# A streaming encoder layer: three groups' down products behind a block's last feature, some down weights split as units of their own, and a final norm at half the spacing

## The chip, the cores and the metric

The kernel runs on one core of one Trainium2 chip. A core has TensorE (PE, the matmul array; PEld is its weight load), VectorE (DVE), ScalarE (ACT), GpSimd (POOL) and SyncE (SP, which here issues nearly all DMAs). They run side by side and wait for each other through semaphores. The metric is device time in microseconds (us) of one execution; lower is better. Three runs of the kernel before gave 2262.98, 2264.62 and 2265.98 us.

## The reference

One layer over 2048 prompt frames and 64 sample frames of width 1024: a norm, an input projection, a gated delta rule on one half of the columns and pooling on the other, an output projection, and a feed-forward part with a last norm. The change touches the feed-forward part and the last norm alone:

```python
def rmsnorm(x, w):
    xf = x.astype(jnp.float32)
    y = xf * lax.rsqrt(jnp.mean(xf * xf, axis=-1, keepdims=True) + EPS)
    return (y * w.astype(jnp.float32)).astype(x.dtype)
...
    h = rmsnorm(x, norm2_w)
    x = x + (jax.nn.silu(h @ w_gate) * (h @ w_up)) @ w_down
...
    y_prompt = rmsnorm(hp, normf_w)
    y_sample = rmsnorm(hs, normf_w)
```

`w_gate` and `w_up` are 1024 x 2816, `w_down` is 2816 x 1024. Frames lie along the free axis of the tiles, model width along the 128 partitions.

## The kernel before, in words

**An order planned ahead.** The kernel text does not issue instructions. Each call is noted by a `Machine` (line 64), which knows an estimated duration for each and at the end (`issue`, line 189) puts all of them in a fixed order for each engine by a list schedule: of what is ready by the estimate, the lowest rank first. The rank is the place in the program text; `machine.boost` moves it forward (`HURRY` by 400 places). A tile of a pool has a tag with a number of buffers; who asks for one too many gets a buffer when the estimate says that its last reader is done. Small side jobs are generators (`Chain`, line 395): each `yield x` lets the next step come `x` us of estimated TensorE time later, and `pump()` between matmuls runs the steps that are due.

**Stages.** The first part of the kernel (to about 940 us) makes the delta-rule and pooling halves, the output projection and the residual x, kept in DRAM as `x2d`. The second part is the feed-forward stage, in three blocks of 704 frames (`NB2`, b = 0, 1, 2), each seen as two halves of 352. The 2816 columns of gate and up are 22 features f of 128 (`NF`), in six groups of 4, 4, 4, 4, 2 and 4 (`FGROUPS`, gi = 0 to 5).

**A feature** (`gate_up`, line 1695) computes gate and up for the two halves at once, with seven products (a Strassen scheme over gate/up rows, frame halves and width halves) in place of eight. Each product is 4 x 3 matmuls of 352 columns: operands are split in two float16 parts, and three cross products are summed. ScalarE copies products out of PSUM (`g`, `u`), VectorE adds others, ScalarE makes the sigmoid in three steps (`hr`), VectorE multiplies. The result is the tile `hr`, with `HRAW` buffers. For groups that go on in Strassen form, ScalarE also sums squares of the result (`esq`).

**A group's down product.** When a group's last feature is done, `factors` (line 1763) takes a scale from the squares (the small matmul `ec`), forms four sums per pair of features (`q`, on GpSimd; on VectorE for the last pair of a block) and splits seven factors per pair in two float16 parts, a ScalarE and a VectorE instruction each. They are put in the tile `hq` of the tag `op`, which has two buffers. `down_strassen` (line 1788) then runs, for each weight unit m, seven products (`dx`, `dy`, `dz`), and VectorE adds each into the tiles `y` (eight tiles, one buffer each, loaded from `x2d` by `new_y`). Units: four for a 4-group, two for the 2-group. In block 0 the groups 0 and 4, and in block 2 the group 5, are done without Strassen in float32r (`plain`, line 570; `down`, line 1751; the split features are then `h3l`, also of the tag `op`).

**Order of the work.** The list `order` (lines 573 to 576) is walked by the main loop (line 1824): feature after feature, and the down products of group gi behind feature `f0 + G + LATER` for the first `LASTD` groups, behind the block's last feature for the others. With `LATER, LASTD = 1, 4` (line 1890) groups 0 to 3 come behind features 5, 9, 13 and 17, groups 4 and 5 behind feature 21.

**Weights.** `plan` lists the weight units in order of use, and `weights_ahead` (line 788) keeps up to four ready. A unit takes buffers of two rings of four (`wsp`, `wsp2`; tiles `ws...` for gate/up, `wsd` for down). In block 0 each gate/up unit is loaded, summed on GpSimd, squared and split on ScalarE and VectorE (`prep_strassen`), and its parts are stored (`due`, `stored`); blocks 1 and 2 load the parts. `prep_down` (line 742) does the same for a Strassen down unit. For groups 1, 2, 3 and 5 the sums were made in the first part of the kernel (`summed`). For the groups 0 and 4, which are plain in block 0, nothing is ready in block 1: the unit's first use there loads two pieces (`wrdt`, `wrdl`), takes squares, a scale (the small matmul `wd`), four GpSimd sums (`wrda`, `wrdb`) and the splits into `wsd`, and stores them (`dn<-wsd`). Block 2 loads them (`wsd<-dn`).

**Between blocks.** `load_h` loads and splits the next block's normed input (`hA`, `hB`). `between` (line 1816) is a chain: the final norm of the block just done (`final_norm`, line 1627, through `rstd`, line 861, and `put_y`, line 1636, which scales y on VectorE and stores it to `out_yT`), then `new_y` for the next block, then the norm statistics of the block after. The steps of the final norm are `LAT_STAT` = 1.63 us apart: for each of two halves eight sums of squares, a pause, and eight stores. The last block has its own `last_norm`.

Of the kernel before, what the change touches and what calls it, by code (L numbers as in the profile page):

```python
# [9 lines left out]
F16 = mybir.dt.float16  # L10
# [8 lines left out]
P = 128  # L19
# [22 lines left out]
N2 = TB2 // 2  # L42
# [329 lines left out]
def hybrid_kernel(ctx, tc, a, o):  # L372
    nc = machine = Machine(tc.nc)
# [74 lines left out]
    cpool, wpool, opool = pool("cpool"), pool("wpool"), pool("opool")  # L448
# [22 lines left out]
    psg = psmm  # L471
# [26 lines left out]
    groups, f0 = [], 0  # L498
# [34 lines left out]
    plan, pres = [], []  # L533
# [12 lines left out]
    for j in range(NBLK):  # L546
        win = [("win", m) for m in range(21)]
        base = len(plan)
        at = 5 + 4 * OUT_AFTER
# [16 lines left out]
    def halves(b, gi):  # L566

        return ((0,), (1,)) if (b, gi) == (NB2 - 1, len(groups) - 1) else ((0, 1),)
# [9 lines left out]
    for op in order:  # L578
        if op[0] == "gu":
            plan.append(("gu", op[2]))  # L580
        else:
            plan += [("dn", m, *groups[op[2]]) for m in range(KT)] * len(halves(*op[1:])) if plain(*op[1:]) else [
                ("ds", m, *groups[op[2]]) for m in range(KT // 2 * groups[op[2]][1] // 4)]
    ready, due, stored = [], [], set()
    state = {"at": 0}
    flat = lambda t: t.rearrange("p q n -> p (q n)").bitcast(F32)
    wq = {}
# [8 lines left out]
    def wsplit(t, raw, n=512, eng=None):  # L596
        nc.scalar.copy(t[:, 0, :n], raw[:, :n])
        (eng or nc.vector).tensor_tensor(out=t[:, 1, :n], in0=raw[:, :n], in1=t[:, 0, :n].bitcast(F32), op=ALU.subtract)

    def prep():  # L600
        key = plan[state["at"]]
        state["at"] += 1
        if key[0] == "pre":
            if not state.get("sampled"):
                return plan.insert(next(i for i in range(state["at"], len(plan)) if plan[i][0] != "pre") + 1, key)
            return pre_sums(*key[1:])
        if key in stored and key[0] in wsd:
            parts = []
            for i in range(2):
                t = wtiles(f"p{i}")[1]()  # L610
                nc.sync.dma_start(out=flat(t), in_=wsd[key[0]][key[1], i])
                parts.append(t)
        elif key[0] == "wl":
            raw, parts = (f() for f in wtiles("l"))
            nc.sync.dma_start(out=raw, in_=wpd[key[1]] if key[2] else a["wout"][key[1]][:, :512])
            wsplit(parts, raw)
        elif key[0] in ("win", "wout"):
            parts = []
            for i in range(2):
                raw, t = (f() for f in wtiles(f"p{i}"))  # L620
                src = a[key[0]][key[1]][:, 512 * i : 512 * i + 512]
                nc.sync.dma_start(out=raw, in_=wpd[key[1]] if key[0] == "wout" and i else src)
                if key == ("win", 0):

                    r3, h3, l3 = (x.rearrange("p (k c) -> p k c", c=P) for x in (raw, t[:, 0], t[:, 1]))
                    nc.gpsimd.memset(l3[:, :, 64:].bitcast(F32), 0.0)
                    nc.scalar.copy(l3[:, :, :64], r3[:, :, :64])
                    nc.scalar.copy(h3[:, :, :64], r3[:, :, :64])
                    tt(h3[:, :, 64:], r3[:, :, 64:], l3[:, :, :64].bitcast(F32), ALU.subtract)
                else:  # L630
                    wsplit(t, raw)
                parts.append(t)
            if len(key) == 2:
                due.append((key, [(wsd[key[0]][key[1], i], t) for i, t in enumerate(parts)]))
        elif key[0] == "dn":
            _, m, f0, G = key
            raw, parts = (f() for f in wtiles("d", m % 2 == 0))
            nc.sync.dma_start(out=raw[:, : G * P], in_=a["wd"][m][:, f0 * P : (f0 + G) * P])
            wsplit(parts, raw, G * P, nc.vector)
        elif key[0] == "ds":  # L640
            parts = prep_down(key, *key[1:])
        else:
            parts = prep_strassen(key)
        ready.append((key, parts))

        while due and due[0][0] != key:
            k, done = due.pop(0)
            for dst, t in done:
                nc.sync.dma_start(out=dst, in_=t if t.dtype == F16 else flat(t))
            stored.add(k)  # L650
# [136 lines left out]

    def weights_ahead():
        while state["at"] < len(plan) and len(ready) < AHEAD + 1:
            if plan[state["at"]][0] in ("gu", "dn") and not wq:  # L790
                return
            prep()

# [64 lines left out]
        mm(ps, ones_r, hi, start=True, stop=False)  # L858
        mm(ps, ones_r, lo, start=False, stop=True)

    def rstd(tag, r, src, subs, pool, ttag, tbufs, eng, psg=psmm):

        for lo, n in subs:
            rs = r[:, lo : lo + n]
            for k in range(KT):
                x = src(k, lo, n)
                if k == 0:
                    act(rs, x, AF.Square)
                else:
                    sq = pool.tile([P, n], F32, tag=ttag, name=f"sq{k}{tag}{lo}", bufs=tbufs)  # L870
                    act(sq[:, :n], x, AF.Square)
                    eng.tensor_tensor(out=rs, in0=rs, in1=sq[:, :n], op=ALU.add)
                yield LAT_STAT
            yield WAIT_STAT
            ps = psg(f"rp{tag}{lo}")
            two = [pool.tile([P, n], F32R, tag=ttag, name=f"{nm}{tag}{lo}", bufs=tbufs)[:, :n] for nm in ("hi", "lo")]
            column_sums(ps[:, :n], rs, *two)
            act(rs, ps[:, :n], AF.Ln, bias=epsc, scale=1.0 / D)
            act(rs, rs, AF.Exp, scale=-0.5)
# [90 lines left out]
    for _ in range(PREPS):  # L970
        prep()
# [5 lines left out]
    at = 0  # L977
# [593 lines left out]
    hq = {}  # L1571

    def load_h(b, names):
        for nm in names:
            for k in range(4):
                t = hq[nm][k]
                if "pool" in wq:
                    raw = wq["pool"].tile([P, N2], F32, tag="t", name=f"xh{nm}{k}_{b}", bufs=TB)
                else:
# [12 lines left out]
    for k in (4, 5, 6, 7, 0, 1, 2, 3):  # L1592
        t = wpool.tile([P, 512], F32, tag="xc", name=f"od{k}", bufs=XBUFS["xc"])
# [19 lines left out]
    f2 = pool("f2", behind=True)  # L1613
# [13 lines left out]
    def final_norm(b, ys):  # L1627
        for i in range(2):
            rf = cpool.tile([P, TB2], F32, tag="r", name=f"rf{b}_{i}")
            src = lambda k, *_: ys[k][:, i]  # L1630
            yield from rstd(f"nf{b}_{i}_", rf, src, [(0, N2)], f2, "t", TB, nc.gpsimd)
            for k in range(KT):
                put_y(b, ys, k, i, rf)
                yield LAT_STAT

    def put_y(b, ys, k, i, rf):
        y = ys[k][:, i]
# [4 lines left out]
    def last_norm(b, ys, i, done):  # L1642
# [3 lines left out]
        def new(nm):  # L1646
            return f2.tile([P, 2, N2], F32, tag="hr", name=nm, bufs=HRAW).rearrange("p s n -> p (s n)")[:, :n] if n > N2 else tmp(nm)[:, :n]

# [37 lines left out]
    def tmp(nm):  # L1686
        return f2.tile([P, N2], F32, tag="t", name=nm, bufs=TB)

# [74 lines left out]
    def factors(b, gi):  # L1763

        f0, G = groups[gi]
        es = einv[b, gi] = f2.tile([P, 6], F32, tag="es", name=f"es{b}_{gi}", bufs=2)
        c = es[:, :1]
        scale_of(c, esq.pop((b, gi))[:, : 2 * G], 2 * G, 2.0**13, psp.tile([P, 512], F32, tag="mm", name=f"ec{b}_{gi}", bufs=PSM), "sqe")
        nc.vector.reciprocal(es[:, 1:2], c)
        t = opool.tile([P, 13 * G // 2, N2], F16, tag="op", name=f"hq{b}_{gi}", bufs=2)  # L1770
        for p in range(G // 2):
            f = f0 + 2 * p
            u, v = h3.pop(f), h3.pop(f + 1)
            low = f2.tile([P, N2], F16, tag="h7", name=f"h7{b}_{f}", bufs=4)
            part = {nm: (t[:, 13 * p + 2 * i], t[:, 13 * p + 2 * i + 1] if i < 6 else low) for i, nm in enumerate(FH)}
            gt = (nc.vector if f + 2 == NF else nc.gpsimd).tensor_tensor
            t3, t2, t4 = (tmp(f"q{i}{b}_{f}") for i in (3, 2, 4))
            for nm, x in (("11", u[:, 0]), ("21", v[:, 0]), ("22", v[:, 1])):
                split16(*part[nm], x, c)
            gt(out=t3, in0=v[:, 1], in1=u[:, 1], op=ALU.subtract)  # L1780
            gt(out=u[:, 1], in0=u[:, 1], in1=u[:, 0], op=ALU.subtract)
            gt(out=t2, in0=v[:, 1], in1=u[:, 1], op=ALU.subtract)
            gt(out=t4, in0=v[:, 0], in1=t2, op=ALU.subtract)
            for nm, x in (("T1", u[:, 1]), ("T2", t2), ("T3", t3), ("T4", t4)):
                split16(*part[nm], x, c)
            h3[f] = part
# [29 lines left out]
    def between(b):  # L1816
# [4 lines left out]
        if b + 2 < NB2:  # L1821
            yield from stats2(b + 2, f2, "t", TB)

    for op in order:
        b = op[1]
        if op[0] == "gu":
            f = op[2]
# [5 lines left out]
            gi = max(g for g, (f0, G) in enumerate(groups) if f0 <= f)  # L1833
# [14 lines left out]
        else:  # L1848
            f0, G = groups[op[2]]
# [36 lines left out]
LAT_SILU = 7.08  # L1886
LAT_STAT = 1.63
LAT_APPLY = 1.69
TB = 7
LATER, LASTD = 1, 4  # L1890
STATS0 = 0
ODB = 200
PREPS = 1
# [3 lines left out]

SLACK = 0.6
TINY = 1e-30
HRAW = 7  # L1900
HOT_ROWS = BOOST
HPOOL = (0, 1, 2, 3)
LAT_LOAD = 0.6
# [115 lines left out]
```

## Time and profile before

| | us |
|---|---|
| median of three runs | 2264.62 |
| lowest and highest | 2262.98, 2265.98 |
| the profiled execution | 2265.8 |
| its span, first to last instruction | 2264.0 |

Mean granted clock of TensorE over the span: 0.994 of full speed.

How to read it: nearly all instructions are recorded by one helper and so carry the line L286; groups are told apart by the names of their tiles, buffer numbers left out. Times in windows and in the chain are us from the span's start. A duration of a matmul in the profile includes its way through the array, and matmuls overlap: the distance from one start to the next is what counts, and the chain shows it. Waits are put down to what ended last.

### The profile page before, as it was taken

Reading aid. Unit: us, or ns where it says so; the run is one execution under the profiler, and the core shown is the slowest. Engines: PE = TensorE matmul, PEld = TensorE weight load, DVE = VectorE, ACT = ScalarE, POOL = GpSimd, SP = SyncE. Lnnn points to the kernel's source line nnn. Section 1 sums busy time; section 2 is a strip of 40 time slices with the busy share of each in tenths; the row PEclk is TensorE's granted clock in tenths of the full one; section 3 lists DMA queues with packets and bytes.
Section 4 is the critical chain, followed back from the end, with each engine's and each line's share of the span. In section 5 each row is a group of like instructions: output and inputs, shape, how many; then the busy total and the mean of one; then the engine's idle time right before and its main releaser. Section 6 shows DMA issues by size and latency. Waiting matters only on the chain. (4 is left out here: it accounts for less than half of the span.)

```text
span 2264.0 us, 41509 instructions
## 1 busy us (share of the span) xinstructions
PE 2207.0 (97%) x14763; PEld 1649.5 (73%) x14763; DVE 1611.4 (71%) x3198; ACT 1437.4 (63%) x3437; POOL 767.0 (34%) x869
## 2 busy tenths in 40 slices
PE   8999999999999999999999999999999999999998
PEld 8998898788878788758666676656666566666667
DVE  8988876685667887788998986666545756445647
ACT  6987876796768875687787775743533554423533
POOL 3425233443236551356444226342200152010102
PEclk9999999999999999999999999999999999999999
DMA  8765477657566667986686567487644576544442
GB/s 304 252 194 185 162 267 244 204 190 240 190 203 219 202 181 237 316 268 224 233 277 202 182 225 250 151 309 223 195 146 154 181 245 206 149 149 148 145 140 70
DMA packets 219392, 467.73 MB, mean 207 GB/s; under 512 B 27184, under 2 KB 88624, under 8 KB 219184
## 3 DMA queue, kind: packets, MB, share of 16 engines
q1 hardware_dynamic: 218608, 464.36, 63.3%
q8 instruction: 115, 1.88, 0.3%
q14 instruction: 93, 0.76, 0.1%
q10 hardware_dynamic: 576, 0.72, 0.1%
HBM read 336.77 MB, written 128.22 MB: 205 GB/s over the span
## 5 line engine op out<-in xcount | busy, mean ns | idle before, releaser
L286 PE MATMUL pp<-h,wsp 128*128 128x512 f32 (+1 forms) x2480 | 546.2, 363 | 8.6 <-DVE wsp L286 8.6
L286 PEld LDWEIGHTS pp<-h,wsp 128*128 128x128 f32 x2480 | 402.3, 189 | 57.4 <-ACT wsp L286 8.6
L286 PEld LDWEIGHTS <-wsd 128*128 128x128 f16 x2352 | 231.1, 99 | 143.1 <-issue 13.7
L286 PE MATMUL dx<-hq,wsd 128*128 128x352 f16 x1232 | 237.6, 316 | 9.5 <-ACT wsd L286 2.8
L286 PEld LDWEIGHTS <-ws11S 128*128 128x128 f16 x1584 | 153.4, 98 | 87.2 <-ACT ws11S L286 5.5
L286 PEld LDWEIGHTS <-wsS3S 128*128 128x128 f16 x1584 | 154.2, 98 | 85.0 <-issue 4.5
L286 PEld LDWEIGHTS <-wsS 128*128 128x128 f16 x1584 | 154.3, 98 | 84.3 <-issue 3.7
L286 DVE SCALAR_TENSOR_TENSOR y<-dx,es,y 128x352 f32<-128x352 f32 x240 | 135.3, 579 | 72.7 <-PE dx L286 68.2
L286 ACT COPY g<-px 128x352 f32<-128x352 f32 x132 | 58.3, 442 | 179.5 <-PE px L286 178.2
L286 PE MATMUL pz<-op,wsp 128*128 128x288 f32 (+1 forms) x768 | 163.0, 353 | 0.3 <-DVE op L286 0.3
L286 ACT ACTIVATE hr<-g,wscale 128x352 f32<-128x352 f32 x132 | 77.1, 584 | 134.9 <-DVE g L286 134.8
L286 POOL TENSOR_TENSOR q<-hr,hr 128x352 f32<-128x352 f32 x52 | 52.3, 1006 | 291.0 <-DVE hr L286 289.4
L286 PE MATMUL px<-hA,ws11S 128*128 128x352 f16 x792 | 137.3, 313 | 4.6 <-ACT ws11S L286 3.6
L286 ACT CAST TV_p<-pt_p 128x512 f16<-128x512 f32 x192 | 109.0, 588 | 42.0 <-PE pt_p L286 41.1
L286 PE MATMUL pz<-hA,wsS 128*128 128x352 f16 x792 | 134.4, 313 | 0.9 <-ACT wsS L286 0.8
L286 PE MATMUL py<-hA,wsS3S 128*128 128x352 f16 x792 | 134.3, 312 | 0.1
L286 PE MATMUL py<-hA,ws11S 128*128 128x352 f16 x792 | 132.8, 313 | 0.5 <-DVE hr L286 0.2
L286 PE MATMUL dy<-hq,wsd 128*128 128x352 f16 x672 | 129.7, 319 | 3.3 <-DMA out_yT_dram<-y 1.6
L286 PE MATMUL px<-hA,wsS 128*128 128x352 f16 x792 | 129.6, 312 | 2.1 <-ACT g L286 2.1
L286 PE MATMUL px<-hB,ws 128*128 128x352 f16 x792 | 129.5, 313 | 2.0 <-DVE u L286 2.0
L286 PE MATMUL px<-hA,wsS3S 128*128 128x352 f16 x792 | 129.6, 313 | 0.7 <-ACT g L286 0.6
L286 PEld LDWEIGHTS pz<-op,wsp 128*128 128x128 f32 x768 | 120.5, 188 | 12.6 <-DVE op L286 0.7
(755 smaller groups left out, 4940.5 us busy)
## 6 DMA issues: line engine op xcount, KB each, us to landing
wsp<-wnd SPq DMA_DIRECT2D x126, 512.0 KB, 3.8
ws11S<-g SPq DMA_DIRECT2D x44, 512.0 KB, 3.9
wsS3S<-g SPq DMA_DIRECT2D x44, 512.0 KB, 3.6
wsS<-g SPq DMA_DIRECT2D x44, 512.0 KB, 3.6
wnd<-wsp SPq DMA_DIRECT2D x42, 512.0 KB, 5.0
wsd<-dn SPq DMA_DIRECT2D x34, 512.0 KB, 3.5
xd<-x2d SPq DMA_DIRECT2D x96, 176.0 KB, 3.5
wsd<-dn SPq DMA_DIRECT2D x34, 384.0 KB, 3.5
```

Of the source, the lines that this page charges most:

```text
L286: getattr(getattr(self.nc, op.eng), name)(*args, **kw)
```

## The change

1. `LASTD` becomes 3: group 3's down products also come behind the block's last feature, ahead of those of groups 4 and 5. Group 4's factors in Strassen form get a tile of their own tag (`hq2`, one buffer), where a third `hq` would be needed. In block 0 group 4 is plain, and its split features stay in the tag `op`.
2. `plan` gets units `pd` behind some features of block 1: the four down units of group 0 behind features 0 to 3, the two of group 4 behind features 7 and 9 (`PREP_AT`). Such a unit is split and stored, and is not handed to TensorE; the unit's use later in block 1 loads it.
3. The final norm of blocks 0 and 1 steps at `PACE` = 0.8 in place of 1.63; the pause stays.
4. Buffers: the small tiles `t` have 8 in place of 7 (`TB`), the features' outputs 6 in place of 7 (`HRAW`).

No matmul is added or taken away.

```diff
     for op in order:
         if op[0] == "gu":
             plan.append(("gu", op[2]))
+            if op[1] == 1 and op[2] in PREP_AT:
+                gi, m = PREP_AT[op[2]]
+                plan.append(("pd", m, *groups[gi]))
...
+        elif key[0] == "pd":
+            key = ("ds", *key[1:])
+            prep_down(key, *key[1:])
+            return
         elif key[0] == "ds":
             parts = prep_down(key, *key[1:])
...
-            if plan[state["at"]][0] in ("gu", "dn") and not wq:
+            if plan[state["at"]][0] in ("gu", "dn", "pd") and not wq:
...
-    def rstd(tag, r, src, subs, pool, ttag, tbufs, eng, psg=psmm):
+    def rstd(tag, r, src, subs, pool, ttag, tbufs, eng, psg=psmm, pace=None):
...
-                yield LAT_STAT
+                yield pace or LAT_STAT
...
-            yield from rstd(f"nf{b}_{i}_", rf, src, [(0, N2)], f2, "t", TB, nc.gpsimd)
+            yield from rstd(f"nf{b}_{i}_", rf, src, [(0, N2)], f2, "t", TB, nc.gpsimd, pace=PACE)
             for k in range(KT):
                 put_y(b, ys, k, i, rf)
-                yield LAT_STAT
+                yield PACE
...
-        t = opool.tile([P, 13 * G // 2, N2], F16, tag="op", name=f"hq{b}_{gi}", bufs=2)
+        t = (f2.tile([P, 13, N2], F16, tag="hq2", name=f"hq{b}_{gi}", bufs=1) if G == 2 else
+             opool.tile([P, 26, N2], F16, tag="op", name=f"hq{b}_{gi}", bufs=2))
...
-TB = 7
-LATER, LASTD = 1, 4
+TB = 8
+LATER, LASTD = 1, 3
...
-HRAW = 7
+HRAW = 6
+PREP_AT = {0: (0, 0), 1: (0, 1), 2: (0, 2), 3: (0, 3), 7: (4, 0), 9: (4, 1)}
+PACE = 0.8
```

## The prediction

> **What bounds the kernel now.** I read the page first, for the share of each engine.
>
> ```profile
> span 2264.0 us, 41509 instructions
> PE 2207.0 (97%) x14763; PEld 1649.5 (73%) x14763; DVE 1611.4 (71%) x3198; ACT 1437.4 (63%) x3437; POOL 767.0 (34%) x869
> ```
>
> TensorE is the bound, and the change takes no matmul away. It can only win time in which TensorE waits or runs slowly. So I went on to the waits of TensorE, window by window over the feed-forward stage (from about 940 us), and kept the four places where they are dense. Columns: who waited, for whom, us in total, times, longest.
>
> ```profile
> PE dz L286 <- DVE y L286: 2.6, 1, 2.6
> PE dx L286 <- DVE hq L286: 0.6, 1, 0.6
> ...
> PE dx L286 <- ACT wsd L286: 2.8, 1, 2.8
> PE px L286 <- DVE u L286: 1.5, 1, 1.5
> PE dx L286 <- DVE wsd L286: 0.7, 1, 0.7
> ...
> PE ec L286 <- DVE sqe L286: 3.1, 1, 3.1
> PE dx L286 <- ACT hq L286: 1.4, 1, 1.4
> ...
> PE dy L286 <- DMA out_yT_dram<-y: 1.6, 1, 1.6
> PE dz L286 <- DVE y L286: 0.6, 1, 0.6
> ```
>
> The places are: the end of block 0 (1361 us on), the first down products of block 1 (1460 on), the end of block 1 (1789 on) and the first down products of block 2 (1910 on). A wait also has a second price, which the windows view shows (PE, PEld, DVE, ACT and POOL busy with counts, granted clock, DMA share, GB/s). Beside it stand one stretch from the chain that ended last, and two rows of the half-clock stretch itself.
>
> ```profile
> 1814.12 2.69 PE dx L286 x18
> ...
> 1361.00:1373.00 12.00, 8.32 (x38) 4.36 (x37) 10.50 (x20) 8.14 (x19) 8.22 (x10) 0.72 0.80 262
> 1367.00:1369.00 2.00, 2.00 (x8) 1.02 (x7) 2.00 (x6) 0.97 (x2) 2.00 (x3) 0.50 0.83 230
> 1460.00:1468.00 8.00, 6.33 (x42) 3.89 (x40) 8.00 (x15) 7.80 (x17) 1.04 (x2) 1.00 0.12 33
> 1474.00:1486.00 12.00, 8.13 (x35) 3.63 (x34) 11.87 (x19) 6.17 (x17) 8.12 (x8) 0.72 0.96 325
> 1789.00:1806.00 17.00, 11.62 (x63) 6.47 (x61) 16.83 (x41) 8.80 (x22) 0.00 (x0) 0.80 0.44 137
> 1910.00:1924.00 14.00, 11.13 (x74) 6.97 (x72) 9.77 (x18) 0.00 (x0) 0.03 (x1) 1.00 0.96 356
> ```
>
> 18 matmuls in 2.69 us is 0.149 us each when nothing waits. What a window lost is its length less its matmuls at 0.149: 12 − 38 × 0.149 = **6.3 us** at the end of block 0; 8 − 42 × 0.149 = 1.7 and 12 − 35 × 0.149 = 6.8, together **8.5**, at the start of block 1; 17 − 63 × 0.149 = 7.6 at the end of block 1, and 8 of those 63 are the `ec` column sums of hardly any length (the other 55 make 8.2 us), so I take **8.5**; 14 − 74 × 0.149 = **3.0** at the start of block 2. In sum 26.3 us. About half of it is the clock: in 1367 to 1369 TensorE is busy throughout and does 8 matmuls where 13 would fit, at a granted clock of 0.50.
>
> [...] Here the longest single wait before a halved clock was 2.6 us, with shorter ones just ahead, while 1910 to 1924 kept 1.00 through shorter waits; the measured windows decide, and they hold both prices already.
>
> **The change, part by part.** *Three groups' products behind the last feature.* The waits at the block ends come from the factors of the last group: they need the last feature's output, and only group 4's products cover them.
>
> ```profile
> 1781.00:1806.00 25.00, 19.62 (x116) 11.71 (x115) 24.67 (x56) 9.16 (x23) 0.00 (x0) 0.86 0.44 144
> ...
> L286 DVE SCALAR_TENSOR_TENSOR y<-dx,es,y 128x352 f32<-128x352 f32 x16 | 8.6, 576 | 0.0
> L286 DVE SCALAR_TENSOR_TENSOR hq<-hr,es,hq 128x352 f16<-128x352 f32 x8 | 4.1, 578 | 0.0
> ...
> L286 ACT ACTIVATE hq<-hr,es 128x352 f16<-128x352 f32 x8 | 4.0, 574 | 0.2 <-DVE es L286 0.2
> ...
> 2223.43 18.89 PE d L286 x117
> ```
>
> At block 1's end VectorE is busy 24.67 of 25 us. One weight unit of a Strassen down product is 7 products of 6 matmuls: 42 × 0.149 = 6.26 us for a unit of a 4-group, 7 additions into y at 8.6 / 16 = 0.54 us. Cover before: two units of group 4, twelve and a half us. After: four units of group 3 more, 25.0, in all 37.6 us. VectorE's work in it: 42 additions (22.6 us), the 14 splits of the factors (0.51 each, 7.2), some 3 us of sums and finishing: 33 us. It fits, ScalarE's 14 splits at 0.5 (7 us) fit far better, and TensorE has work throughout. I take the whole **8.5 us** there; bounds 0 and 8.5.
>
> At block 0's end the cover is 25.0 us of group 3 and group 4's plain products: 96 matmuls at 18.89 / 117 = 0.161, 15.5 us. But here the change adds a wait. The tag `op` has two buffers; group 3's factors and group 4's split features hold both, so the last group's 14 splits can only be written when TensorE has read group 3's factors for the last time. Their instructions on ScalarE and VectorE stand in an order fixed ahead, and what is queued behind them, the copies out of PSUM and the additions into y, would wait too if group 3 came late. From there 15.5 us remain, and VectorE has 7.2 us of splits and 16 additions (8.3 us at about 0.52, estimated from the 0.54 above): 15.5 against 15.5. The splits rank first, and nothing of the column sum is left to do then, so the first product should start in time and later ones wait a little. Bounds: 0 and 6.3 us left; I take 2 left, **4.3 won**. In blocks 1 and 2 group 4 has its own buffer, and nothing waits.
>
> The price is a run of eight features (14 to 21) without down products between. In blocks 1 and 2 that is free. In block 0 ScalarE and VectorE also split each feature's weights:
>
> ```profile
> 1311.00:1336.00 25.00, 25.00 (x176) 16.47 (x175) 20.51 (x41) 22.31 (x53) 6.48 (x7) 1.00 0.61 216
> ...
> L286 ACT ACTIVATE junk<-wr 128x512 bf16<-128x512 f32 x9 | 5.6, 622 | 5.2 <-DMA wr<-in_wg_dram 5.2
> L286 ACT CAST wsd<-wrd 128x256 fp32r<-128x256 f32 x7 | 2.7, 401 | 2.6 <-PE pz L286 1.3 <-PE py L286 1.3
> ...
> PE px L286 <- ACT ws11S L286: 1.8, 1, 1.8
> PE dx L286 <- ACT hq L286: 1.0, 1, 1.0
> ...
> 940.00:1025.00 85.00, 77.37 (x524) 49.29 (x523) 74.90 (x126) 76.70 (x174) 42.82 (x32) 1.00 0.86 297
> ```
>
> Two features (25 us) with the splits of two weight units take 22.3 us of ScalarE; in a steady run six more squares (0.62 each, 3.7) come and four casts for group 4 (1.6) go: about 24.5 of 25. Eight features are 100 us, two units are ready ahead (some 15 us of ScalarE saved), group 3's 14 splits come in (7). So ScalarE just keeps up, with some 10 us in hand over 100. The features' worst wait for weights in the rest of block 0 was 1.8 us. The bound from the other side is the run of six features at the stage's start: 85 − 77.4 = 7.6 us idle at this load with the stage change on top. I take 2 us new, less the 1.0 that TensorE now waits for group 3's factors: **1 us lost**; bounds 1 won and 7.6 lost. One buffer fewer for the features' outputs costs nothing: six hold one group and two features more.
>
> *Weights of groups 0 and 4 as units of their own.* Before, group 0's four units are made between feature 5 and their use; after, one behind each of features 0 to 3 of block 1, and loaded back.
>
> ```profile
> L286 POOL TENSOR_TENSOR wrda<-wrdt,wrdl x6: 727/773/1082, 1358.0 to 1516.0; 128x256 f32<-128x256 f32 x6
> L286 DVE SCALAR_TENSOR_TENSOR wsd<-wrdt,dscale,wsd x6: 741/752/1418, 1449.3 to 1769.2; 128x512 f16<-128x512 f32 x6
> dn<-wsd SPq DMA_DIRECT2D x6, 512.0 KB, 4.9
> wsd<-dn SPq DMA_DIRECT2D x34, 512.0 KB, 3.5
> ...
> 1396.00:1471.00 75.00, 73.22 (x499) 47.73 (x498) 44.01 (x83) 55.22 (x130) 31.18 (x35) 1.00 0.52 161
> ```
>
> A unit is four POOL sums (3.1 us), four splits on VectorE (about 3) and on ScalarE with two squares (about 4), two loads, two column sums, two stores. The 75 us before the stall have room for what is moved in: VectorE 44, ScalarE 55, POOL 31, DMA at 0.52. What is added is twelve loads (six of 512 KB, six smaller) in SP's queue at 3.5 us to landing, well ahead of use. With the weights there, the 2.8 and 0.7 us waits go; so does the congestion of VectorE (11.87 of 12 us). What may be late next is group 0's own factors; I leave 1.5 us. **7.0 us won**, bounds 0 and 8.5. Group 4's two units saw no wait, and moving them earlier gives nothing.
>
> *Final norm at half the spacing.* Two halves of 16 steps, each 0.83 us closer: 26.6 us sooner at the end.
>
> ```profile
> 1853.98 0.87 SPq L286 DMA_DIRECT2D out_yT_dram<-y  x2
> 1907.59 0.98 SPq L286 DMA_DIRECT2D out_yT_dram<-y  x2
> 1909.21 5.47 SPq L286 DMA_DIRECT2D y<-x2d  x6
> ```
>
> The last store goes out at 1907.6 and the next y is fetched at 1909 to 1915, while TensorE needs it from 1910. Stores at about 1881 free y long before: **3.0 us won**, bounds 0 and 3.0. In block 1 y is late too, behind the late weights, and this edit is what keeps it from being the next wait there. The buffer more for small tiles only relieves.
>
> **Sum.** 8.5 + 4.3 − 1 + 7.0 + 3.0 = 21.8 us. The profiled execution took 2265.8 us (span 2264.0 and 1.8 around it) and becomes 2244.0; the median of the three runs is 2264.62, 1.2 us lower, so I say **2243 us**.
>
> **The rivals.** *ScalarE-bound run* (13%): block 0's eight features lose 7.6 us and not 1; gain 15.2, 2249 us. For it: the 24.5 of 25 above; against: two units ahead, and waits of at most 1.8 us before.
>
> *Crowded start of block 1* (8%): the norm's sums and the weights' sums meet on POOL, VectorE's operations on two SBUF inputs slow down, and the 7.0 are not won: gain 14.8, 2250 us. Against it: POOL is busy 31 of 75 us. [...]
>
> *The wait only slides* (5%): the last groups' factors are late behind all three groups, at both ends, because VectorE falls behind its 33 of 37.6 us. 12.8 us are not won: gain 9, 2255.6.
>
> *All gains eaten by smaller waits* (5%): no measurable change.
>
> *The new units starve the features* (8%, slower): each holds one of four buffers of both weight rings until its store lands, 4.9 us after issue; if the next feature's weights are then late, TensorE waits as it did for `wsd` (2.8 us) and loses as much again to the clock (6.8 in that window with 3.5 of waits, so 3.3). 6.1 × 6 units = 37 us, less the 22 won: 2280 us. It decides from 21.8 / 6 = 3.6 us per unit. Against it: three buffers remain, a feature needs two and gives the first back after two of seven products.
>
> **How the numbers follow.** The forecast has 61%. A measurement of this kernel can tell about 0.2%, 4.5 us, from no change. Faster: 61 + 13 + 8 + 5 = 87%; within 0.2%: 5%; slower: 8%. The range goes from everything won, 26.3 us and the 1.0 of group 3, with a little for rounding (2236), to the sliding wait (2256).
>
> **What would show it.** Right: at block 1's end no `ec` or `hq` wait and a clock of 1.00; no `wsd` wait and no `out_yT_dram` wait; granted clock near 1.00 in all slices from 1300 us on. Wrong: new `ws11S` or `g` waits of TensorE between features 16 and 21 of block 0 (the ScalarE-bound run), weight-tile waits behind features 1 to 4 of block 1 (starved), `hq` waits behind group 4 in block 0 beyond 2 us. The forecast fails if block 0 loses over 8 us, or if waits of 2.6 us and more, with their clock, come back elsewhere.

## The result, and the profile after

The changed kernel takes 2247.74 us (median of 4 runs, 2245.82 to 2250.57) beside 2265.3 us (4 runs) for the kernel before. The ratio is 0.9921, 95% interval 0.9901 to 0.9940: faster by 0.8%. The forecast was 2243, the range 2236 to 2256.

The page of the changed kernel, its first lines:

```profile
span 2248.7 us, 41466 instructions
PE 2204.6 (98%) x14763; PEld 1651.4 (73%) x14763; DVE 1619.4 (72%) x3198; ACT 1434.8 (64%) x3437; POOL 765.8 (34%) x869
```

The matmuls are the same 14763; the span is 15.3 us shorter. The windows view over the run of eight features and over the four places of the prediction (block 1's end and block 2's start now come 9 and 18 us earlier). The first row is the kernel before in the run of eight features, all others are the changed kernel:

```profile
1245.00:1275.00 30.00, 28.89 (x203) 18.68 (x201) 27.64 (x57) 26.66 (x59) 5.87 (x6) 1.00 0.78 271
...
1245.00:1275.00 30.00, 24.70 (x177) 15.79 (x176) 26.40 (x47) 26.76 (x64) 14.68 (x12) 1.00 0.66 239
1361.00:1373.00 12.00, 11.37 (x73) 9.11 (x72) 12.00 (x24) 9.38 (x23) 10.81 (x11) 1.00 0.88 281
1460.00:1468.00 8.00, 8.00 (x56) 5.28 (x54) 6.84 (x13) 7.63 (x19) 4.26 (x5) 1.00 1.04 387
1474.00:1486.00 12.00, 12.00 (x83) 7.88 (x81) 8.43 (x16) 4.05 (x12) 4.17 (x5) 1.00 0.70 229
1780.00:1792.00 12.00, 8.82 (x38) 4.51 (x37) 10.80 (x23) 8.35 (x19) 7.98 (x10) 0.72 0.70 213
1892.00:1906.00 14.00, 14.00 (x96) 9.18 (x95) 9.21 (x18) 2.26 (x6) 3.73 (x4) 1.00 0.43 136
```

Block 0's end is nearly full (11.37 of 12 us) and the starts of blocks 1 and 2 are full, at a clock of 1.00. The end of block 1 is not: 12 − 38 × 0.149 = 6.3 us are still lost, at a clock of 0.72. And between 1245 and 1275 TensorE is idle for 5.3 us, where the kernel before had 1.1. TensorE's waits, first in the run of eight features (1240 to 1300), then at block 1's end (1745 to 1795):

```profile
PE px L286 <- ACT g L286: 6.3, 5, 1.5
...
PE dx L286 <- DVE y L286: 1.4, 1, 1.4
PE dy L286 <- DVE hq L286: 0.8, 1, 0.8
PE dx L286 <- DVE hq L286: 0.7, 1, 0.7
```

For all kernels of this study I worked out from the traces what TensorE lost at each place: for each matmul the distance from its start to the next one's, less the usual distance of its kind (0.149 us for the 352-column ones), summed over a stretch. Waits and the halved clock are both in it. Bounds set a little differently shift a place's figure by up to 1 us. Single profiled executions differ by several us in the first part of the kernel, which no edit here touches (the first feature starts at 942.2 us in the trace of before and at 946.4 in that of the changed kernel); the places below are compared without it. The kernels were measured in four batches. The kernel before had medians of 2266.8 to 2267.0 us in the three later ones (numbers 1 to 4, 6 to 9, and 5, 10 and 11), 1.6 us above the 2265.3 of the first, so medians of different batches compare to 2 us or so, and the ratios are the safer comparison. One run of number 4 (3195 us) and one of number 9 (7975 us) fell in a slow state and are left out.

| kernel | median us | ratio to before, interval | block 0, features 6 to 21 | block 0 end | block 1 start | block 1 end | block 2 start |
|---|---|---|---|---|---|---|---|
| before | 2265.3 | 1 | 9.4 | 6.8 | 9.8 | 8.8 | 3.4 |
| changed | 2247.7 | 0.9921, 0.9901 to 0.9940 | 12.3 | 1.3 | 0.9 | 6.5 | 0.0 |
| 1: three es buffers | 2244.9 | 0.9897, 0.9880 to 0.9914 | 12.4 | 1.2 | 0.6 | 4.2 | 0.0 |
| 2: group 3 back | 2243.4 | 0.9892, 0.9875 to 0.9909 | 5.7 | 4.2 | 0.3 | 7.9 | 0.1 |
| 3: no own units | 2250.8 | 0.9929, 0.9909 to 0.9948 | 12.1 | 1.2 | 3.5 | 10.0 | 0.0 |
| 4: norm at 1.63 | 2261.5 | 0.9973, 0.9963 to 0.9983 | 12.3 | 1.2 | 9.9 | 6.7 | 5.1 |
| 5: the move and buffers alone | 2265.7 | 0.9997, 0.9986 to 1.0007 | 12.5 | 1.3 | 12.8 | 8.6 | 5.3 |
| 6: 1, and group 3 back in block 0 | 2240.6 | 0.9889, 0.9872 to 0.9906 | 5.7 | 5.5 | 0.4 | 2.5 | 0.0 |
| 7: 6, and factors without head start | 2237.4 | 0.9877, 0.9860 to 0.9893 | 5.5 | 4.8 | 0.4 | 0.0 | 0.0 |
| 8: buffers alone | 2263.3 | 0.9985, 0.9972 to 0.9997 | 5.7 | 1.4 | 11.4 | 8.8 | 5.0 |
| 9: norm and buffers alone | 2247.5 | 0.9917, 0.9896 to 0.9938 | 5.5 | 2.2 | 3.5 | 8.9 | 0.1 |
| 10: eight small tiles alone | 2262.6 | 0.9972, 0.9955 to 0.9990 | 5.6 | 5.3 | 12.9 | 8.6 | 4.3 |
| 11: 7, own units a feature later | 2242.4 | 0.9885, 0.9871 to 0.9900 | 5.7 | 4.8 | 7.7 | 0.2 | 0.0 |

### The profile page after: what moved, and what is told of

It reads as the page before. It is cut to its first block, busy times and chain, and to the rows that moved or that the text cites. A ratio compares the mean times of both kernels' runs of the same rounds, so it can differ in the third digit from the quotient of the medians.

```text
span 2248.7 us, 41466 instructions
## 1 busy us (share of the span) xinstructions
PE 2204.6 (98%) x14763; PEld 1651.4 (73%) x14763; DVE 1619.4 (72%) x3198; ACT 1434.8 (64%) x3437; POOL 765.8 (34%) x869
## 4 chain that ended last, share of the span: by engine, by line
PE 79%; DVE 7%; ACT 6%; issue 3%; DMA 3%; POOL 1%; SPq 0%; DVEq 0%; POOLq 0%; ACTq 0%
PE px L286 17%; PE pp L286 16%; PE pz L286 10%; PE dx L286 9%; PE py L286 8%; PE dy L286 4%; PE d L286 3%; PE dz L286 2%; PE pt_p L286 2%; PE pk_p L286 1%; PE gr_p L286 1%; PE py_p L286 1%; DVE hq L286 1%; DVE y L286 1%; DVE hr L286 1%
## 5 line engine op out<-in xcount | busy, mean ns | idle before, releaser
L286 PE MATMUL dx<-hq,wsd 128*128 128x352 f16 x1232 | 232.9, 314 | 2.6 <-DVE y L286 1.4
L286 PE MATMUL dy<-hq,wsd 128*128 128x352 f16 x672 | 124.9, 314 | 0.8 <-DVE hq L286 0.8
```

The source lines that it names most:

```text
L286: getattr(getattr(self.nc, op.eng), name)(*args, **kw)
```

## The experiments

Diffs are against the changed kernel, except number 10, which is against the kernel before. Those of 6, 7 and 11 show only what is added to the version that the heading names.

**1. Three es buffers.** The small tile `es` holds a group's scale and the factors of its units. It has two buffers, and the change puts three groups in flight. The instructions of ScalarE in the changed kernel (timeline: start, length, what, idle before and what ended it) show the scale of block 1's last group:

```profile
1772.27 0.49 ACT L286 CAST hA<-xhT 128x352 f16<-128x352 f32 x1 [5.53 <-DMA xhT<-hpd]
1775.71 0.26 ACT L286 ACTIVATE es<-ec,tiny 128x1 f32<-128x1 f32 x1 [2.96 <-DVE y L286]
```

Its column sum was done long before, as TensorE's timeline has it:

```profile
1755.30 0.34 PE L286 MATMUL ec<-sqe,onesb 128*128 128x1 bf16 x8
```

So the scale was written 20 us late, released by an addition into y: group 3's last reader of its `es`. The first splits start at 1776.75, a few us ahead of their use at 1780.

```diff
-        es = einv[b, gi] = f2.tile([P, 6], F32, tag="es", name=f"es{b}_{gi}", bufs=2)
+        es = einv[b, gi] = f2.tile([P, 6], F32, tag="es", name=f"es{b}_{gi}", bufs=3)
```

> The changed kernel with three buffers in place of two for the small tile es, which holds a group's scale and its unit factors. Theory (the third group in flight waits for a scale tile): in the changed kernel the scale of block 1's last group is written only when group 3's additions have released a buffer, 20 us after its column sum, so the group's splits start too late. With three buffers the splits start right behind the column sum, the loss at block 1's end (6.5 us in the changed kernel's trace) falls below 1 us, and the time to about 2241 to 2243. Rival (VectorE has no room behind the last feature, whatever is free): the loss stays between 5 and 7 us and the time at 2246 to 2250.

Measured: 2244.9 us, 4.2 us left at block 1's end. The scale now follows its column sum at once (timeline of ScalarE in this kernel):

```profile
1752.51 0.26 ACT L286 ACTIVATE es<-ec,tiny 128x1 f32<-128x1 f32 x1 [2.87 <-PE ec L286]
1752.80 0.20 ACT L286 ACTIVATE es<-es 128x1 f32<-128x1 f32 x1
1753.22 2.03 ACT L286 ACTIVATE hq<-hr,es 128x352 f16<-128x352 f32 x4 [0.22 <-DVE es L286]
```

The wait for `es` is shown, but its removal won only 2.3 of the 6.5 us. What is late next is in the waits and the windows of the same kernel:

```profile
PE dx L286 <- DVE y L286: 2.4, 1, 2.4
...
1754.00:1762.00 8.00, 5.80 (x39) 3.69 (x38) 7.90 (x16) 7.96 (x18) 1.51 (x2) 1.00 0.57 183
1762.00:1766.00 4.00, 3.83 (x17) 2.10 (x17) 3.30 (x8) 1.94 (x4) 4.00 (x6) 0.64 0.72 213
```

By the order of the program VectorE takes the 14 splits in one go, since they rank 400 places ahead; the additions into y, which empty the PSUM banks that TensorE writes its products to, stand behind them, and TensorE waits. Experiment 7 tests this.

**2. Group 3 back behind feature 17,** the rest of the change kept.

```diff
-LATER, LASTD = 1, 3
+LATER, LASTD = 1, 4
```

> The changed kernel with group 3's down products back behind feature 17 (LASTD = 4), the rest of the change kept. Theory (the move is worth what the traces differ by at its places): the losses at the ends of block 0 and 1 come back (6.6 and 8.9 us for 1.3 and 6.5), the run of eight features in block 0 loses 9.4 for 12.3, in sum about 5 us slower than the changed kernel, 2252 to 2254. Rival (the move is worth nothing beside the weights and the norm, its price in block 0 eats it): within 2 us of the changed kernel.

Measured: 2243.4 us, not slower but 4.4 us faster than the changed kernel by the medians (the two intervals just overlap). Both accounts missed: features 6 to 21 of block 0 lost 5.7 us, not the 9.4 of before. The waits over 1240 to 1310 hold none above half a us; the row for `g` shrinks from 6.3 to

```profile
PE px L286 <- ACT g L286: 0.2, 1, 0.2
```

So the move of group 3's products is a loss in block 0, and something else in the change had made block 0 better (experiments 8 and 10).

**3. No units of their own.**

```diff
-PREP_AT = {0: (0, 0), 1: (0, 1), 2: (0, 2), 3: (0, 3), 7: (4, 0), 9: (4, 1)}
+PREP_AT = {}
```

> The changed kernel without the units of their own (the weights of groups 0 and 4 are made at their first use in block 1, as before). Theory (late weights made the wait at the start of block 1): the wsd waits come back there and with them a halved clock, 5 to 8 us slower than the changed kernel, 2253 to 2256. Rival (the early final norm alone cured that place, since it took the norm's work off VectorE in that stretch and had y there in time): within 2 us of the changed kernel. At block 1's end nothing should change unless group 4's units, made late again, are missed there: up to 3 us more.

Measured: 2250.8 us, 3.1 us slower by the medians and 1.8 by the ratios, whose intervals overlap. In the traces two places lose more. The start of block 1 loses 3.5 us and not 9.8; of the `wsd` waits little is left (waits, 1400 to 1500):

```profile
PE dx L286 <- DVE y L286: 1.5, 2, 0.8
PE dy L286 <- DVE hr L286: 0.6, 1, 0.6
PE dx L286 <- ACT wsd L286: 0.3, 1, 0.3
PE dx L286 <- DVE wsd L286: 0.2, 1, 0.2
```

The rival was the better account of that place. At block 1's end group 4's units are missed: 10.0 us for 6.5.

**4. The final norm at the old spacing.**

```diff
-PACE = 0.8
+PACE = 1.63
```

> The changed kernel with the final norm at the old spacing of 1.63. Theory (the norm's end frees y): at the start of block 2 the wait for the store of y comes back, 3.0 to 3.4 us, and in block 1, where the weights are no longer late, the same wait for y shows for the first time, some 3 us: 5 to 7 us slower than the changed kernel, 2253 to 2255. Rival (y was hidden in block 1 also without the faster norm): 3 us slower, with nothing new at the start of block 1.

Measured: 2261.5 us, 13.8 us slower, twice what was expected. The weights are there, and TensorE still waits at the start of block 1, now for y by name. The waits of TensorE over 1400 to 1500, then SP's issues and VectorE's first addition into the new y (timeline) at the same place:

```profile
PE dz L286 <- DVE y L286: 6.3, 1, 6.3
```

```profile
1473.26 0.33 SPq L286 DMA_DIRECT2D out_yT_dram<-y  x1
1473.68 0.39 SPq L286 DMA_DIRECT2D y<-x2d  x1
1474.21 0.37 SPq L286 DMA_DIRECT2D out_yT_dram<-y  x1
1474.63 6.07 SPq L286 DMA_DIRECT2D y<-x2d  x7
...
1479.90 0.58 DVE L286 SCALAR_TENSOR_TENSOR y<-dx,es,y 128x352 f32<-128x352 f32 x1 [1.93 <-DMA y<-x2d]
```

The last stores of the old y go out at 1474 and the new y is fetched until 1481: VectorE's first addition for group 0 waits for that load, and until the additions run no PSUM bank comes free for TensorE's next `dz`.

**5. The move and the buffers alone** (no own units, norm at 1.63).

```diff
-PREP_AT = {0: (0, 0), 1: (0, 1), 2: (0, 2), 3: (0, 3), 7: (4, 0), 9: (4, 1)}
-PACE = 0.8
+PREP_AT = {}
+PACE = 1.63
```

> The kernel before with the change's buffers and group 3's down products behind the last feature; the norm at the old spacing, no units of their own. Theory (the move loses in block 0 and, with two buffers for es, wins nothing at block 1's end): features 6 to 21 of block 0 lose 12 us in place of 5.5 with the buffers alone, block 1's end 9 to 10 as without the move, so 6 to 9 us slower than the buffers alone (2263.3): 2268 to 2273, at or above the kernel before. Rival (the prediction's own account: cover at both block ends is worth 12.8 us less 1): 2255 to 2259.

Measured: 2265.7 us, ratio 0.9997 (0.9986 to 1.0007): no gain over the kernel before, and 2.4 us above the buffers alone (number 8; the intervals overlap); less than the 6 to 9 expected, though the five places together lose 8.2 us more in the traces. The prediction's own account (2255 to 2259) is far off. Features 6 to 21 lose 12.5 us as forecast, block 1's end 8.6.

**6. Group 3 back in block 0 alone, added to the three es buffers of number 1.**

```diff
-... if f == (min(f0 + G + LATER, NF - 1) if gi < LASTD else NF - 1)]
+... if f == (min(f0 + G + LATER, NF - 1) if gi < LASTD + (b == 0) else NF - 1)]
```

> Three buffers for es as in the run before, and in block 0 alone group 3's down products back behind feature 17; blocks 1 and 2 keep them behind the last feature. Theory (the run of eight features in block 0 costs more than the move wins there): with group 3's products back, the features 6 to 21 of block 0 lose 5.5 us in place of 12.3 and the end of block 0 4.1 in place of 1.3, as in the run with LASTD = 4, so 4 us better than es alone (2244.9): 2240 to 2242. Rival (the loss in the run of eight is noise of the order, and the cover at block 0's end is worth its 3 us): 2244 to 2248.

Measured: 2240.6 us, as the theory had it; by the ratio to before it is 1.8 us better than experiment 1, within the intervals. The traces show it at its places: block 0's features lose 5.7 us for 12.4, its end 5.5 for 1.2.

**7. Number 6, and the factors of blocks 1 and 2 without their head start.**

```diff
-                    machine.boost = HURRY if f == NF - 1 else 0
+                    machine.boost = HURRY if f == NF - 1 and b == 0 else 0
```

> The same, and in blocks 1 and 2 the factors of the last group are no longer put 400 places ahead in rank. Theory (with two groups' products as cover nobody needs these factors soon, and their 14 splits in one go keep VectorE from emptying PSUM: the 4.2 us left at block 1's end with es alone): the loss there falls below 1.5 us, 3 us better than the run beside it: 2236 to 2239. Rival (VectorE has no room in that stretch in any order): the same loss, a little later, and the same time as the run beside it within 1.5 us.

Measured: 2237.4 us, ratio 0.9877 (0.9860 to 0.9893). Block 1's end loses nothing, in the window in which experiment 1 lost its 2.4 us:

```profile
1743.00:1770.00 27.00, 27.00 (x190) 17.77 (x188) 25.83 (x53) 13.54 (x31) 10.70 (x12) 1.00 0.65 218
```

VectorE is busier there than in experiment 1 (23.39 us in the same window), so what changed is the order, and not its load. This version beats both kernels: its interval lies below that of the changed kernel. Against experiment 6 the intervals overlap, and the traces tell them apart (2.5 us are lost at block 1's end there). Of what is left, one wait at block 0's end (1340 to 1400) is long, and the timelines of TensorE and ScalarE show what stands behind it:

```profile
PE dz L286 <- ACT dscale L286: 2.6, 1, 2.6
```

```profile
1368.58 0.19 PE L286 MATMUL wd<-sqb,onesb 128*128 128x1 bf16 x2
...
1369.10 0.48 ACT L286 CAST hA<-xh 128x352 f16<-128x352 f32 x1 [1.34 <-DMA xh<-hpd]
1370.03 0.63 ACT L286 ACTIVATE junk<-wrdt 128x512 bf16<-128x512 f32 x1 [0.44 <-DMA wrdt<-in_wd_dram]
1371.03 0.25 ACT L286 ACTIVATE dscale<-wd,tiny 128x1 f32<-128x1 f32 x1
```

The first own unit's column sum `wd` is done at 1368.8. ScalarE reads it at 1371.0, because a cast and the squares of the second unit's weights stand ahead in its order and wait for loads (1.34 and 0.44 us). Until it is read, `dz` has no PSUM bank.

**8. The buffers alone** (group 3 behind feature 17, no own units, norm at 1.63).

```diff
-PREP_AT = {0: (0, 0), 1: (0, 1), 2: (0, 2), 3: (0, 3), 7: (4, 0), 9: (4, 1)}
-PACE = 0.8
-LATER, LASTD = 1, 3
+PREP_AT = {}
+PACE = 1.63
+LATER, LASTD = 1, 4
```

> The kernel before with the buffers of the change alone (small tiles t 8 in place of 7, feature outputs 6 in place of 7, group 4's factors in a tile of their own); order, units and norm as before. Theory (the eighth small tile is what made block 0 lose less in the run with LASTD = 4): features 6 to 21 of block 0 lose 5.5 us in place of 9.4 and its end 4.1 in place of 6.6; 4 to 6 us faster than before, 2259 to 2262. Rival (that came with the order of the instructions that follow): within 2 us of before.

Measured: 2263.3 us, ratio 0.9985 (0.9972 to 0.9997), a gain of 3.4 us (0.7 to 6.3) where 4 to 6 were expected. Block 0 loses 5.7 and 1.4 in place of 9.4 and 6.8, and the two later starts take part of it back: block 1's loses 11.4 in place of 9.8, block 2's 5.0 in place of 3.4. At block 1's start TensorE's long waits now have other names than `wsd` (1400 to 1500):

```profile
PE dz L286 <- DVE hr L286: 3.1, 1, 3.1
PE dz L286 <- DVE y L286: 2.8, 1, 2.8
```

**9. The norm and the buffers alone.**

```diff
-PREP_AT = {0: (0, 0), 1: (0, 1), 2: (0, 2), 3: (0, 3), 7: (4, 0), 9: (4, 1)}
-LATER, LASTD = 1, 3
+PREP_AT = {}
+LATER, LASTD = 1, 4
```

> The kernel before with the change's buffers and its faster final norm, nothing else. Theory (y that came late was behind most of the wait at the start of block 1 too; the weights' waits stood in front of it): the start of block 1 loses 3 to 4 us in place of 9.5, the start of block 2 nothing in place of 3.4; 9 to 10 us faster than the buffers alone, 2248 to 2251. Rival (the weights are the wait at the start of block 1, as the trace of before names them): the loss there stays at 7 us or more, only 3 to 4 us faster than the buffers alone.

Measured: 2247.5 us (three runs), ratio 0.9917 (0.9896 to 0.9938): what the whole change gives. The start of block 1 loses 3.5 us, that of block 2 nothing, as expected. By the ratios the gain over the buffers alone is some 15 us, more than the 9 to 10 expected; the five places lose 12.1 us less.

**10. Eight small tiles alone,** against the kernel before.

```diff
-TB = 7
+TB = 8
```

> The kernel before with eight small tiles t in place of seven, nothing else. Theory (the eighth tile is what took the losses of block 0 down in the run with the buffers alone): features 6 to 21 of block 0 lose 5.5 us in place of 9.4 and block 0's end about 1 in place of 6.6, time 2259 to 2264. Rival (the other two buffer edits did it, or only the changed order): losses as before and the time within 2 us of before.

Measured: 2262.6 us, ratio 0.9972 (0.9955 to 0.9990). Features 6 to 21 lose 5.6 us: the eighth tile is what helps there, be it by waits that it spares or by the order that the list schedule makes of it; the runs do not separate the two. Block 0's end lost 5.3 and not about 1. In the runs with `LASTD` = 4 in block 0 that place lost between 1.4 and 5.5, mostly by one wait for `y` of 0.7 or some 3 us; which order of instructions gives which was not found.

**11. The best version (number 7), own units one feature later.**

```diff
-PREP_AT = {0: (0, 0), 1: (0, 1), 2: (0, 2), 3: (0, 3), 7: (4, 0), 9: (4, 1)}
+PREP_AT = {1: (0, 0), 2: (0, 1), 3: (0, 2), 4: (0, 3), 7: (4, 0), 9: (4, 1)}
```

> The best version so far (three es buffers, block 0 with LASTD = 4, factors of blocks 1 and 2 without their head start) with group 0's four units one feature later each, behind features 1 to 4 in place of 0 to 3. Theory (the first unit's column sum holds a PSUM buffer at block 0's end until its late weights are squared, and TensorE waits 2.6 us for dscale there): that wait goes, 2 to 3 us better than the version beside it (2237.4): 2234 to 2236. Rival (the wait only moves with the unit, or the later units come late for group 0): the same time within 1.5 us, or a wsd wait at the start of block 1.

Measured: 2242.4 us, 5 us slower than the version beside it by the medians, 1.8 by the ratios, whose intervals overlap; in the traces the start of block 1 loses 7.7 us for 0.4. The `dscale` wait is gone, though the weights that the theory called late were those of the second unit, as the timeline in experiment 7 shows; two other waits are there (waits, 1340 to 1460), of which that for `y` is the one of some 3 us at block 0's end again:

```profile
PE px L286 <- DMA ws11S<-g: 3.7, 1, 3.7
PE dz L286 <- DVE y L286: 3.1, 1, 3.1
```

A feature's weights come 3.7 us late at 1441. The chain around it shows why:

```profile
1435.48 4.06 DMA dn<-wsd
...
1439.56 5.76 DMA ws11S<-g
```

The load of the weights is issued only when the store of an own unit has landed and given its buffer back: the slower rival of the prediction, in one instance.

## Why the prediction was right, and where it was not

The direction and the range held, and the size in the main: the places won 17.2 us in the traces and 17.6 by the medians, where 21.8 were forecast. Block 1's end was taken 6.2 us too high and the price of the run of features 1.9 too low; the other three terms were 1.2, 1.9 and 0.4 too low and make up for part of it. The 1.9, at block 1's start, is luck: that place was won by another cause than the one named.

- **Block 1's end, 8.5 us won: 2.3 measured (8.8 to 6.5).** The failed step is "TensorE has work throughout. I take the whole 8.5 us there", with "in blocks 1 and 2 group 4 has its own buffer, and nothing waits". I looked for shared buffers under `op` alone. The scale tile `es` has two as well, and kept the splits back for 20 us of the 37.6 us of cover; this is shown by the instruction that released the scale and by experiment 1, in which 2.3 us of the 6.5 went. VectorE's work did fit, as the 33 of 37.6 us said, but not in the order given: the head start of the factors stopped the additions (experiments 1, 6 and 7).
- **The start of block 1, 7.0 us won by the units; block 2, 3.0 by the norm.** The sums came out (8.9 and 3.4 measured), the cause named for block 1 did not; the total was right there by luck. The trace of before named `wsd`, and I gave that place to the weights. Experiments 4 and 9 show that y was late there too: beside the buffers the faster norm takes the place from 11.4 to 3.5 us, while the units without it take it only from 12.8 (experiment 5) to 9.9 (experiment 4). The text said that the norm "is what keeps it from being the next wait there"; what that sentence left without a number was the larger term. The units are worth the last 2.6 us (3.5 to 0.9) there.
- **"Moving them earlier gives nothing"** (group 4's units): without any own units block 1's end loses 3.5 us more (experiment 3).
- **Block 0's run of eight features, 1 us lost: 2.9 measured (9.4 to 12.3),** and the price of the move itself is 6.6 to 6.8, from 5.5 to 5.7 without it: nearly the 7.6 of the rival. The eighth small tile hid the difference. "The buffer more for small tiles only relieves" was costed at nothing and is worth some 4 us. That the price came out small is luck too. The sign that the prediction gave for its ScalarE-bound run came, new `g` waits (6.3 us) in features 16 to 18, and ScalarE is where they arise. Its timeline in the changed kernel shows the PSUM copy `g` behind a weight split and a factor split:

```profile
1266.18 0.72 ACT L286 ACTIVATE ws<-wr,wscale 128x512 f16<-128x512 f32 x1 [0.98 <-PE px L286]
1266.81 0.57 ACT L286 ACTIVATE hq<-hr,es 128x352 f16<-128x352 f32 x1
1267.29 0.43 ACT L286 COPY g<-px 128x352 f32<-128x352 f32 x1
```

  TensorE resumes 0.5 us after that copy starts, after 1.4 us of waiting. The weights themselves were in time; what I had not looked for is that the copies out come late first. It is not only load: ScalarE was idle for 0.98 us just before, and it was as busy in the same window of the kernel before (26.66 us of 30, now 26.76). The splits stand ahead of the copy in its fixed order. How much is load and how much order was not tested.
- **Block 0's end, 4.3 won: 5.5 measured (6.8 to 1.3).** But experiments 8 and 9 reach 1.4 and 2.2 there without the move, so the move's part of it is not settled.
- **The rivals.** The sliding wait was right for block 1's end, with the scale's buffer and the order in place of VectorE's load as its cause. The crowded start did not come: 0.9 us lost there in the changed kernel. The slower operations that it counted on are in the trace of before: VectorE's `wsd<-wrdt`, with both inputs in SBUF, took 1.42 us at 1478.2, where GpSimd was at work on a norm's sums (`r<-r,sq2n`, 1.09 us), and 0.74 us at 1464.3, where GpSimd was idle. Starved features came only in experiment 11.
- **A reading of the rows.** That "the longest single wait before a halved clock was 2.6 us" is true of block 0's end alone: the prediction's own rows have 2.8 us (`wsd`) at block 1's start and 3.1 (`sqe`) at block 1's end, each just ahead of the half clock there. No term hangs on it.

Taken together: the norm and the buffers alone give what the whole change gives. The move of three groups loses in block 0 about what it and the units win elsewhere in the traces, until the scale tile, the head start and block 0 are mended (2237.4 us).

## What to carry to other kernels

When a change puts one more item in flight, count the buffers of every tile that the item holds, the smallest too: a tile of six columns with two buffers held a group's work back by 20 us, and what was late behind it showed only when it was mended. A wait that the trace names may stand in front of another of the same length; test each of the two causes alone before dividing the gain between them. And work that is urgent while nothing covers it should lose its priority when the cover comes, or it delays what has become urgent.

## What the runs showed of the hardware

In the changed kernel the clock fell to 0.50 without any single long wait. At block 1's end TensorE had waited 0.3, 0.7 and 0.8 us between 1780.4 and 1783.3, and the clock fell at 1783.4, within the first of these rows; its wait of 1.4 us came only behind that.

```profile
1782.00:1784.00 2.00, 1.12 (x5) 0.34 (x4) 2.00 (x5) 2.00 (x6) 0.00 (x0) 0.85 0.53 170
...
1785.00:1790.00 5.00, 4.75 (x17) 2.49 (x17) 4.22 (x9) 2.79 (x7) 5.00 (x7) 0.50 0.75 219
```

And one wait of 2.4 us at the same place was followed by a clock of 0.64 in experiment 1 (1762 to 1766, above), but by 1.00 in experiment 6:

```profile
1757.00:1761.00 4.00, 3.51 (x24) 2.32 (x24) 4.00 (x9) 2.09 (x5) 4.00 (x6) 1.00 0.77 242
```

So waits below one us alone stood ahead of a halved clock at block 1's end, 1.8 us of them within some 3 us. The same wait of 2.4 us cost 1.7 us more in experiment 1 than in experiment 6 (4.2 and 2.5 us lost at that place); why the clock fell in the one and not in the other was not shown. In the clock records of the kernel before and of the changed kernel, between 1200 and 2200 us, there are four stretches at half clock, from 1365.0, 1477.6 and 1798.5 us in the one and from 1783.4 us in the other. Each lasted 6.8 us, and TensorE was idle for 1.9, 2.8, 3.4 and 1.8 of the 4 us ahead of it.
